# A hybrid decoder trunk on one core: weights stationary for the lora, k, r and v projections, three rounded passes for r1, v and the A blocks

## The chip, the cores and the metric

One core of a Trainium2 chip. The metric is the device time of one execution in microseconds; the median of three runs before the change is 2560.14 us (2558.58 to 2572.45). Engine names in the rows: PE is TensorE's matmul, PEld its weight load, DVE is VectorE, ACT ScalarE, POOL GpSimd, SP SyncE, which here only issues transfers.

## The reference

256 positions of width 2048 go through two layers. Layer 0 is what the change touches:

```python
h = rmsnorm(x, g_pre_mix) * (1 + sc_m) + sh_m      # shift/scale from c @ w_ada ("adaLN")
z = h @ w_in_ab                                    # 2048 -> 2*1024 (A: u, v) + 5 parts for B
y_a = chunked_spatial_gating(z[..., :2048], ...)   # gelu, layernorm of v, 128x128 causal mixing
y_b = rwkv7_time_mix(z[..., 2048:], ...)           # r, k, v of 1024; lora parts of 64, 64, 160
y = concatenate([y_a, y_b]) @ w_out_ab
x = x + gt_m * rmsnorm(y, g_post_mix)
```

`rwkv7_time_mix` begins with a token shift, `z + mu * (z_prev - z)`, where `z_prev` is z one position earlier. Then decay, gates and a delta-rule state update over the positions follow. Each layer has a SwiGLU feed-forward behind it, layer 1 has attention in place of A and B. All is in 32-bit floats.

## The kernel before, in words

**Ways to multiply.** A *rounded* matmul uses fp32r operands: a 32-bit value is split into a rounded high half and a rest, and a product is made of three passes (high x high, high x low, low x high). `load_split` loads one step of weights (256 rows of K by 512 columns, 512 KB, buffers `w32`, four of them) and splits it: a copy on ScalarE (`wh`, line 191) and a subtraction on VectorE (`wl`, line 192), both issued at a raised priority. `dense` multiplies so. `dense32` (line 893) multiplies the same step with plain floats, `xT` stationary and the weights moving, and splits nothing. One plain-float matmul shows as two records in the trace, a rounded one as one.

**First stage (lines 410 to 469).** x comes transposed (`xT`, features on partitions). Shift and scale of the pre-norm are dots of `cond` (silu of c on every partition) with strips of `w_ada`, 1 MB each: `strips(j)` loads four of them through six scratch buffers in turn (`slots`) and VectorE dots each with `cond` (`ada_dot`, line 117), giving the shift and scale of two K tiles. `h_rows(j)` applies them on ScalarE. Then the weights of lora (288 columns), k0, k1 and r0 for these two K tiles are loaded into two sets of scratch buffers (`wslots`) and multiplied into eight banks of PSUM. j runs from 0 to 7. All these transfers go through SP's queue in the order of the program; x, `cond` and the small tables come through ScalarE's queue. Position lies on the partitions of the results, so ScalarE copies them to scratch (`zn_tiles`, line 469).

**Second stage.** The main stream is seven blocks of `dense32`, eight steps each: r1, v0, v1 (the rest of B), then two blocks of A's v and two of A's u; then `w_out` for A's half (4 blocks of 4 steps, `dense`), and after that for B's half. A background generator, `rk_gen`, holds all of B's work in pieces, each with a credit; `pump`, called after every step, releases pieces at 1.8 credits a step (3 in its last part) and one or more adaLN strips of later sublayers (`ada_gen`, 512 KB each, two buffers, one dot on VectorE each). The piece order of `rk_gen`: lora transposes and shift (line 495), sigmoids and decay (`E`), `to_T("k")`, key normalisation, `to_T("r")`, bonus, `to_T("v")`, scores `SCN` and `SRA`, a triangular inversion of 31 sequential steps on VectorE (lines 669 to 674), then the four chunks of the state update and group norm, ending in `YB`. `to_T` (line 527) transposes a block of k, r or v on TensorE, 128 by 128 (line 539), and applies the token shift: a scaled copy on ScalarE and one or two multiply-adds on VectorE. The second half of `w_out` needs `YB`.

**Order.** The framework lays instructions out engine by engine before the run, by priority (program order, with the splits raised) among what its own estimate holds ready; on the chip each engine and each queue then runs its list strictly in order. Big scratch tiles share slots by tag: `H0`, `H1` and `X` hold one tile each at a time, a new owner waiting for the old one's last reader.

Of the kernel before, what the change touches and what calls it, by code (L numbers as in the profile page):

```python
# [7 lines left out]
F32 = mybir.dt.float32  # L8
F32R = mybir.dt.float32r
# [42 lines left out]
def trunk(ctx: ExitStack, tc, io, out, dbg=None):  # L52
# [32 lines left out]
    om = cpool.tile([P, 27], F32, name="om")  # L85
    V.tensor_scalar(om, cols[:, COLS["mu_k"][0]:COLS["mu_l"][1]], -1.0, 1.0, op0=OP.mult, op1=OP.add)
    oka = cpool.tile([P, 8], F32, name="oka")
    V.tensor_scalar(oka, cols[:, COLS["k_a"][0]:COLS["k_a"][1]], -1.0, 1.0, op0=OP.mult, op1=OP.add)

# [271 lines left out]
    def split_from(ps_ap, h_ap, l_ap):  # L361
# [4 lines left out]
    EX = hpool.tile([P, KT, S], F32, tag="H0", name="EX")  # L366
# [18 lines left out]
    EXf = EX.rearrange("p k s -> p (k s)")  # L385
    slots = [KBf[:, 0:D], KBf[:, D:2 * D], SCf[:, 0:D], SCf[:, D:2 * D], EXf[:, 0:D],
             EXf[:, D:2 * D]]
# [4 lines left out]

# [3 lines left out]
    def nat(flat_ap, i, ncol):  # L396
        return flat_ap[:, i:i + NT * ncol].rearrange("p (t n) -> p t n", t=NT)

    lora, win = io["w_lora"], io["w_in"]
    zn_tiles = {"lora": nat(ATf, 0, 288), "k0": nat(RAf, 2048, 512), "k1": nat(RAf, 3072, 512),  # L400
                "r0": nat(RAf, 0, 512), "r1": nat(RAf, 1024, 512),
                "v0": nat(VTf, 0, 512), "v1": nat(VTf, 1024, 512)}
# [5 lines left out]
    with tc.tile_pool(name="spool", bufs=1) as sp:  # L408
# [30 lines left out]
        def h_rows(j, cc):  # L439
            for k in range(2):  # L440
                kt = 2 * j + k
                A.activation(xT[:, kt, :], xT[:, kt, :], AF.Identity, bias=cc[:, 0, k:k + 1],
                             scale=cc[:, 1, k:k + 1])

        def bank(pool, nm):
# [5 lines left out]
               "r0": [bank(ps_ms, "ms") for _ in range(NT)]}  # L451
        for j in range(KT // 2):
            cc = strips(j)
            if j == 0:
                for k4 in range(4):
                    ks = slice(4 * k4, 4 * k4 + 4)
                    V.tensor_tensor(xT[:, ks, :], xT[:, ks, :], rb4, op=OP.mult)
# [20 lines left out]
    E = hpool.tile([P, 2, 8, S], F32, tag="H0", name="E")  # L478
    have = {"lora", "k0", "k1", "r0"}
# [6 lines left out]
    def rk_gen():  # L486

        while "lora" not in have:
            yield None
        zn = zn_tiles["lora"]  # L490
        zl = lp.tile([P, 3, S], F32, tag="gbu", name="zl")
        for f, w in ((0, P), (1, P), (2, 32)):
            ps = msbank()
            for t in range(NT):
                T.transpose(ps[:w, tsl(t)], zn[:, t, f * P:f * P + w], ident)
            A.activation(zl[:w, f, :], ps[:w, :S], AF.Copy, scale=omu("l", f)[:w])
            V.scalar_tensor_tensor(zl[:w, f, 1:S], ps[:w, 0:S - 1], col("mu_l", f)[:w],
                                   zl[:w, f, 1:S], op0=OP.mult, op1=OP.add)
            yield 0.8
# [27 lines left out]
        def to_T(name, dst):  # L527
            for b in range(2):
                while f"{name}{b}" not in have:
                    yield None  # L530
                zn = zn_tiles[f"{name}{b}"]
                pss = []
                for i2 in range(2):
                    ps = msbank()
                    psv = ps.rearrange("p (g s) -> p g s", g=2)
                    for i in range(2):
                        f = 2 * i2 + i
                        for t in range(NT):
                            T.transpose(psv[:, i, tsl(t)], zn[:, t, f * P:(f + 1) * P], ident)
                    pss += [psv[:, 0], psv[:, 1]]  # L540
                for i in range(4):
                    g, z = 4 * b + i, pss[i]
                    mu = col("mu_" + name, g)
                    if name == "k":
                        A.activation(dst[:, g], c4(z), AF.Copy, scale=omu(name, g))
                        V.scalar_tensor_tensor(dst[:, g, 0, 1:64], z[:, 0:63], mu,
                                               dst[:, g, 0, 1:64], op0=OP.mult, op1=OP.add)
                        V.scalar_tensor_tensor(dst[:, g, 1:4, :],
                                               z[:, 63:255].rearrange("p (c t) -> p c t", c=3), mu,
                                               dst[:, g, 1:4, :], op0=OP.mult, op1=OP.add)  # L550
                    else:
                        A.activation(dst[:, g, :], z, AF.Copy, scale=omu(name, g))
                        V.scalar_tensor_tensor(dst[:, g, 1:S], z[:, 0:S - 1], mu, dst[:, g, 1:S],
                                               op0=OP.mult, op1=OP.add)
                    if i % 2:
                        yield 0.8

        R_, Kk = RA[:, 0], RA[:, 1]
        K_, B_ = KB[:, :, :, 0, :], KB[:, :, :, 1, :]

        def c4(a):
            return a.rearrange("p (c t) -> p c t", c=4)

        yield from to_T("k", K_)


# [30 lines left out]
        yield from to_T("r", R_)  # L597
# [19 lines left out]
        yield from to_T("v", VT)  # L617
# [5 lines left out]
        SRA = hpool.tile([P, 64, 64], F32, tag="H1", name="SRA")  # L623
# [255 lines left out]
        YB = hpool.tile([P, 2, 8, S], F32R, tag="H1", name="YB")  # L879
# [13 lines left out]
    def dense32(wsrc, evac):  # L893
        ps = [ps_mm.tile([P, 512], F32, name="mm") for _ in range(NT)]
        for ch in range(KT // 2):
            w = wpool.tile([P, 2, 512], F32, tag="w32", name="w32", bufs=4)
            SY.dma_start(w, wsrc(ch))
            for k in range(2):
                kt = 2 * ch + k
                for t in range(NT):  # L900
# [5 lines left out]
    def evac_z(nm):  # L906
        def f(ps):
            for t in range(NT):
                A.activation(zn_tiles[nm][:, t, :], ps[t], AF.Copy)
            have.add(nm)  # L910
        return f

    for nm, src, ncol in first[4:]:
        dense32(src, evac_z(nm))
# [383 lines left out]
```

## Time and profile before

| | |
|---|---|
| median of 3 runs | 2560.14 us (2558.58 to 2572.45) |
| the profiled execution | 2557.72 us, its span 2555.7 us |
| TensorE matmul busy | 2429.3 us, 95% of the span |
| TensorE weight load busy | 1860.5 us, 73% |
| VectorE busy | 1619.6 us, 63% |
| ScalarE busy | 1037.1 us, 41% |
| GpSimd busy | 102.0 us, 4% |
| transfers | 623.47 MB, mean 244 GB/s |

The trace's times are microseconds from the start of the span. A window's row gives how long each engine was busy in it. A group's row gives a line of the kernel, the engine, the operation, tiles out<-in with their shapes, how many there were, their busy time, the mean length of one in ns, and the engine's idle time just before them with what ended it. Matmuls are pipelined, so the length of one is not its pace: the pace is read from starts, or from a merged run of them.

### The profile page before, as it was taken

The page shows a single profiled execution, that of the slowest core. Times are in us where ns is not written, and L with a number is a line of the kernel's source. Part 1 is how long each engine was busy: PE and PEld are TensorE (multiplying, and loading weights), DVE is VectorE, ACT ScalarE, POOL GpSimd, SP SyncE. Part 2 cuts the span into 40 slices and gives each one's busy share as a digit, 9 for nine tenths or more (in the row PEclk, how much of TensorE's full clock was granted, in tenths as well). Part 3 has the DMA queues.
Part 4 walks back from the last instruction along what each step waited for, and adds up shares of the span by engine and source line. Part 5 has one row for each costly group of instructions (what it writes and reads, how often), then busy time and mean ns, then how long its engine had stood idle before and what let it go on. Part 6 is the DMA issues. An engine that isn't in the chain of part 4 may idle for free. (4 is left out here: it accounts for less than half of the span.)

```text
span 2555.7 us, 29570 instructions
## 1 busy us (share of the span) xinstructions
PE 2429.3 (95%) x10944; PEld 1860.5 (73%) x10944; DVE 1619.6 (63%) x2176; ACT 1037.1 (41%) x1423; POOL 102.0 (4%) x83
## 2 busy tenths in 40 slices
PE   4998989998999999999998999999899999999998
PEld 2443537677887777888887777778778888888886
DVE  5656794568877777654446778865776455444444
ACT  1042103347443443444445444446544444444443
POOL 0002210001000000000001001100100000000000
PEclk8998999899999999999999999999999999999999
DMA  9987776574988888755554888855587555556554
GB/s 377 417 302 242 259 245 212 177 265 146 329 317 306 317 296 310 234 205 191 193 193 146 302 292 311 300 196 206 201 318 265 188 190 189 189 190 206 191 194 151
DMA packets 166528, 623.47 MB, mean 244 GB/s; under 512 B 18560, under 2 KB 18752, under 8 KB 161392
## 3 DMA queue, kind: packets, MB, share of 16 engines
q1 hardware_dynamic: 164288, 612.74, 68.7%
q10 hardware_dynamic: 2096, 8.86, 0.9%
q8 instruction: 85, 1.39, 0.2%
q14 instruction: 59, 0.48, 0.1%
HBM read 619.39 MB, written 2.13 MB: 243 GB/s over the span
## 5 line engine op out<-in xcount | busy, mean ns | idle before, releaser
L192 DVE TENSOR_TENSOR wl<-w,wh 128x1024 fp32r<-128x1024 f32 x688 | 836.8, 1223 | 532.9 <-ACT wh L191 531.7
L191 ACT ACTIVATE wh<-w 128x1024 fp32r<-128x1024 f32 x688 | 728.3, 1059 | 1005.4 <-PE mm L205 941.7
L117 DVE SCALAR_TENSOR_TENSOR ada<-ada,cond 128x1024 f32<-128x1024 f32 x320 | 392.9, 1229 | 286.1 <-DMA ada<-in_w_ada_dram 285.2
L204 PE MATMUL mm<-wl,hF 128*128 128x512 f32 x1408 | 552.4, 392 | 15.0 <-DVE wl L192 14.8
L203 PE MATMUL mm<-wh,hF 128*128 128x512 f32 x1408 | 552.9, 393 | 0.0
L205 PE MATMUL mm<-wh,hFl 128*128 128x512 f32 x1408 | 549.9, 391 | 0.0
L204 PEld LDWEIGHTS mm<-wl,hF 128*128 128x128 f32 x1408 | 264.5, 188 | 81.8 <-DVE wl L192 28.6
L205 PEld LDWEIGHTS mm<-wh,hFl 128*128 128x128 f32 x1408 | 264.4, 188 | 54.5
L203 PEld LDWEIGHTS mm<-wh,hF 128*128 128x128 f32 x1408 | 264.5, 188 | 53.7
L204 PE MATMUL mm<-wl,aH 128*128 128x512 f32 x704 | 276.9, 393 | 0.0
L205 PE MATMUL mm<-wh,aL 128*128 128x512 f32 x704 | 275.5, 391 | 0.0
L203 PE MATMUL mm<-wh,aH 128*128 128x512 f32 x704 | 274.6, 390 | 0.0
L901 PE MATMUL mm<-w,xT 128*128 128x512 f32 x448 | 216.3, 630 | 4.6 <-DMA w<-in_w_in_dram 4.6
L901 PEld LDWEIGHTS mm<-w,xT 128*128 128x128 f32 x448 | 86.2, 201 | 105.9 <-issue 97.7
L203 PE MATMUL mm<-wh,hA 128*128 128x512 f32 x384 | 155.7, 405 | 0.0
L204 PE MATMUL mm<-wl,hA 128*128 128x512 f32 x384 | 152.3, 397 | 3.1 <-DVE wl L192 3.1
L203 PEld LDWEIGHTS mm<-wh,aH 128*128 128x128 f32 x704 | 132.2, 188 | 30.1
L204 PEld LDWEIGHTS mm<-wl,aH 128*128 128x128 f32 x704 | 132.3, 188 | 28.6
L205 PEld LDWEIGHTS mm<-wh,aL 128*128 128x128 f32 x704 | 132.3, 188 | 27.7
L205 PE MATMUL mm<-wh,hAl 128*128 128x512 f32 x384 | 150.8, 393 | 0.0
L204 PEld LDWEIGHTS mm<-wl,hA 128*128 128x128 f32 x384 | 72.8, 190 | 20.1 <-DVE wl L192 6.3
L205 PEld LDWEIGHTS mm<-wh,hAl 128*128 128x128 f32 x384 | 72.7, 189 | 15.1
(312 smaller groups left out, 2049.5 us busy)
## 6 DMA issues: line engine op xcount, KB each, us to landing
w<-in_w_ffn_in_dram SPq DMA_DIRECT2D x352, 512.0 KB, 3.9
ada<-in_w_ada_dram SPq DMA_DIRECT2D x320, 512.0 KB, 5.1
w<-in_w_ffn_out_dram SPq DMA_DIRECT2D x176, 512.0 KB, 3.6
w<-in_w_qkv_dram SPq DMA_DIRECT2D x96, 512.0 KB, 5.2
w<-in_w_in_dram SPq DMA_DIRECT2D x56, 512.0 KB, 5.2
w<-in_w_out_dram SPq DMA_DIRECT2D x32, 512.0 KB, 3.8
w<-in_w_o_dram SPq DMA_DIRECT2D x32, 512.0 KB, 3.3
KB<-in_w_ada_dram SPq DMA_DIRECT2D x12, 1024.0 KB, 12.0
```

Source lines behind the costliest of these rows:

```text
L117: V.scalar_tensor_tensor(w, w, 1.0, cond[:, k0:k0 + n], op0=OP.mult, op1=OP.mult, accum_out=dst)
L191: A.activation(wh[:, :, :ncol], w32[:, :, :ncol], AF.Copy)
L192: V.tensor_sub(wl[:, :, :ncol], w32[:, :, :ncol], wh[:, :, :ncol].bitcast(F32))
L203: T.matmul(o, h, wh[:, k, :ncol], start=(kt == 0), stop=False)
L204: T.matmul(o, h, wl[:, k, :ncol], start=False, stop=False)
L205: T.matmul(o, l, wh[:, k, :ncol], start=False, stop=(kt == nkt - 1))
L901: T.matmul(ps[t], xT[:, kt, tsl(t)], w[:, k, :], start=(kt == 0), stop=(kt == KT - 1))
```

## The change

- Lora, k0, k1 and r0 are multiplied with the weights stationary, in pieces of 128 columns (lora 128, 128, 32), and `xT` moving, 256 positions wide. So columns land on partitions, and the token shift reads PSUM directly (`shift`, `shift4`, and a loop for lora). `to_T`, the transposes, `zn_tiles` and the copies to them are gone. The shifts of lora, k and r0 stand before the background generator, which then waits for r1 and v1 only.
- r1, v0 and v1 become `dense_T`: weights split by `load_split` and stationary, `XH` and `XL` (the split of h, made in `h_rows`) moving, 256 columns, three rounded passes.
- The four A blocks become `dense` with three rounded passes of 512 columns.
- `strips(0)` stands before the loop and `strips(j+1)` before the weights of set j. There are five strip buffers instead of six.
- Two small operations on the column table (`om`, `oka`) move behind the first stage; scratch tiles change tags (`XH`, `XL` take `H0`, `H1`; `E`, `SRA`, `YB` go to `X`; `YA` to `H0`, `YP` to `H1`).

```diff
-    EX = hpool.tile([P, KT, S], F32, tag="H0", name="EX")
...
-    slots = [KBf[:, 0:D], KBf[:, D:2 * D], SCf[:, 0:D], SCf[:, D:2 * D], EXf[:, 0:D],
-             EXf[:, D:2 * D]]
+    slots = [KBf[:, 0:D], KBf[:, D:2 * D], SCf[:, 0:D], SCf[:, D:2 * D], ATf]
...
+            ks = slice(2 * j, 2 * j + 2)
+            A.activation(XH[:, ks, :], xT[:, ks, :], AF.Copy)
+            V.tensor_sub(XL[:, ks, :], xT[:, ks, :], XH[:, ks, :].bitcast(F32))
...
+        nxt = strips(0)
...
         for j in range(KT // 2):
-            cc = strips(j)
...
+            cc = nxt
             h_rows(j, cc)
+            if j + 1 < KT // 2:
+                nxt = strips(j + 1)
             for i, (nm, src, ncol) in enumerate(first[:4]):
                 w = wslots[j % 2][i][:, :2 * ncol].rearrange("p (k n) -> p k n", k=2)
                 SY.dma_start(w, src(j))
+                nf = -(-ncol // P)
                 for k in range(2):
                     kt = 2 * j + k
-                    for t in range(NT):
-                        T.matmul(acc[nm][t][:, :ncol], xT[:, kt, tsl(t)], w[:, k, :],
-                                 start=(kt == 0), stop=(kt == KT - 1))
-        for nm, src, ncol in first[:4]:
-            for t in range(NT):
-                A.activation(zn_tiles[nm][:, t, :ncol], acc[nm][t][:, :ncol], AF.Copy)
+                    for f in range(nf):
+                        n = min(P, ncol - f * P)
+                        T.matmul(acc[nm][f // 2][:n, (f % 2) * S:(f % 2 + 1) * S],
+                                 w[:, k, f * P:f * P + n], xT[:, kt, :],
+                                 start=(kt == 0 and f % 2 == 0),
+                                 stop=(kt == KT - 1 and (f % 2 == 1 or f == nf - 1)))
...
+        else:
+            A.activation(dst[:, g, :], z, AF.Copy, scale=omu(name, g))
+            V.scalar_tensor_tensor(dst[:, g, 1:S], z[:, 0:S - 1], mu, dst[:, g, 1:S],
+                                   op0=OP.mult, op1=OP.add)
...
+    def dense_T(wsrc, name, b):
+        ps = [ps_mm.tile([P, 512], F32, name="mm") for _ in range(2)]
         for ch in range(KT // 2):
-            w = wpool.tile([P, 2, 512], F32, tag="w32", name="w32", bufs=4)
-            SY.dma_start(w, wsrc(ch))
+            wh, wl = load_split(wsrc(ch), 512)
             for k in range(2):
                 kt = 2 * ch + k
-                for t in range(NT):
-                    T.matmul(ps[t], xT[:, kt, tsl(t)], w[:, k, :], start=(kt == 0),
-                             stop=(kt == KT - 1))
+                for f in range(4):
+                    o = ps[f // 2][:, (f % 2) * S:(f % 2 + 1) * S]
+                    fs = slice(f * P, (f + 1) * P)
+                    T.matmul(o, wh[:, k, fs], XH[:, kt, :], start=(kt == 0 and f % 2 == 0),
+                             stop=False)
+                    T.matmul(o, wh[:, k, fs], XL[:, kt, :], start=False, stop=False)
+                    T.matmul(o, wl[:, k, fs], XH[:, kt, :], start=False,
+                             stop=(kt == KT - 1 and f % 2 == 1))
             pump(AR, BR)
-        evac(ps)
...
+        shift4(name, b, ps, tgt[name])
+        have.add(f"{name}{b}")
...
-        dense32(src, evac_z(nm))
+        dense_T(src, nm[0], int(nm[1]))
...
-        dense32(lambda ch, b=b: win[6 + b, ch], evac_av(b))
+        dense(lambda ch, b=b: win[6 + b, ch], KT, *hl(XH, XL), 512, evac_av(b), AR, BR)
...
-        dense32(lambda ch, b=b: win[8 + b, ch], evac_au(b))
+        dense(lambda ch, b=b: win[8 + b, ch], KT, *hl(XH, XL), 512, evac_au(b), AR, BR)
```

## Rows read from the trace of the kernel before

**Rows 1.** Windows: length, busy PE PEld DVE ACT POOL, PEclk, DMA share, GB/s.
```profile
57.87:134.30 76.43, 73.87 (x193) 36.23 (x191) 47.63 (x50) 5.89 (x12) 0.00 (x0) 1.00 1.00 408
134.30:146.65 12.35, 12.35 (x33) 6.19 (x33) 3.97 (x7) 4.25 (x8) 0.52 (x1) 1.00 0.91 329
146.65:312.40 165.75, 156.07 (x512) 77.56 (x510) 110.47 (x215) 49.53 (x94) 29.63 (x31) 0.95 0.76 259
312.40:381.50 69.10, 57.40 (x129) 24.74 (x129) 62.96 (x120) 6.20 (x10) 13.65 (x6) 0.96 0.75 252
381.50:500.00 118.50, 116.32 (x1104) 77.01 (x1105) 59.64 (x101) 40.77 (x69) 0.00 (x0) 0.88 0.60 197
500.00:553.00 53.00, 49.10 (x280) 39.27 (x279) 42.14 (x66) 20.68 (x28) 0.00 (x0) 0.94 0.70 240
```

**Rows 2.** Waits of TensorE, 146 to 500: us in total, times, longest.
```profile
PE ms L690 <- DVE AT L683: 9.3, 2, 7.1
...
PE mm L901 <- DMA w<-in_w_in_dram: 4.6, 2, 2.4
```

**Rows 3.** Timeline of TensorE: start, length, operation, count [idle before, releaser].
```profile
158.47 2.75 PE L511 MATMUL ms<-tz,w2a 128*128 128x256 f32 x12
...
171.38 10.46 PE L901 MATMUL mm<-w,xT 128*128 128x512 f32 x24
181.68 1.04 PE L539 MATMUL ms<-cst,RA 128*128 128x128 f32 x8
...
397.61 2.05 PE L958 MATMUL ms<-vA,wsT 128*128 128x128 f32 x16
...
526.85 0.39 PE L203 MATMUL mm<-wh,YA 128*128 128x512 f32 x1
...
529.57 0.39 PE L203 MATMUL mm<-wh,YA 128*128 128x512 f32 x1
```

**Rows 4.** Groups by shape, 146.65 to 553: busy, mean ns, idle before.
```profile
L117 DVE SCALAR_TENSOR_TENSOR ada<-ada,cond 128x1024 f32<-128x1024 f32 x107 | 132.1, 1239 | 90.8 <-DMA ada<-in_w_ada_dram 90.4
...
L192 DVE TENSOR_TENSOR wl<-w,wh 128x1024 fp32r<-128x1024 f32 x14 | 16.8, 1217 | 3.2 <-ACT wh L191 3.2
L191 ACT ACTIVATE wh<-w 128x1024 fp32r<-128x1024 f32 x15 | 15.8, 1056 | 22.4 <-PE mm L205 14.4 <-DMA w<-in_w_out_dram 5.7 <-DVE ada L117 2.3
...
L958 PEld LDWEIGHTS ms<-vA,wsT 128*128 128x128 f32 x32 | 3.8, 191 | 0.4 <-issue 0.3
...
L545 ACT ACTIVATE KB<-ms,om 128x256 f32<-128x256 f32 x8 | 3.5, 466 | 7.4 <-DVE KB L548 7.4
...
L548 DVE SCALAR_TENSOR_TENSOR KB<-ms,cols,KB 128x192 f32<-128x192 f32 x8 | 3.3, 408 | 0.0
...
L884 DVE TENSOR_TENSOR YB<-RA,YB 128x512 fp32r<-128x512 f32 x4 | 2.5, 687 | 0.2 <-ACT YB L883 0.2
```

**Rows 5.** Timeline of VectorE and GpSimd in the inversion.
```profile
330.32 0.34 DVE L672 TENSOR_TENSOR AT<-AT,KBn 128x175 f32<-128x175 f32 x1
...
360.04 4.20 POOL L942 TENSOR_TENSOR vA<-vA,gn 128x1024 f32<-128x1024 f32 x1 [41.50 <-DVE vA L941]
...
361.96 2.48 DVE L672 TENSOR_TENSOR AT<-AT,KBn 128x175 f32<-128x175 f32 x1
```

**Rows 6.** Timeline of the first stage, TensorE and VectorE.
```profile
23.75 0.18 DVE L86 TENSOR_SCALAR om<-cols 128x27 f32<-128x27 f32 x1 [22.68 <-DMA cols<-in_cols_dram]
...
43.05 4.21 PE L465 MATMUL ms<-RA,xT 128*128 128x288 f32 x8 [17.06 <-ACT xT L442]
...
57.87 2.10 PE L465 MATMUL ms<-vA,xT 128*128 128x288 f32 x8
...
108.94 2.29 DVE L117 SCALAR_TENSOR_TENSOR KB<-KB,cond 128x2048 f32<-128x2048 f32 x1 [4.45 <-DMA KB<-in_w_ada_dram]
...
119.78 2.21 PE L465 MATMUL ms<-RA,xT 128*128 128x288 f32 x8 [0.55 <-ACT xT L442]
...
123.53 2.29 DVE L117 SCALAR_TENSOR_TENSOR EX<-EX,cond 128x2048 f32<-128x2048 f32 x1 [4.44 <-DMA EX<-in_w_ada_dram]
...
134.30 2.21 PE L465 MATMUL ms<-vA,xT 128*128 128x288 f32 x8 [2.02 <-ACT xT L442]
...
138.08 1.23 DVE L117 SCALAR_TENSOR_TENSOR ada<-ada,cond 128x1024 f32<-128x1024 f32 x1 [4.46 <-DMA ada<-in_w_ada_dram]
```

More of the change, by code (lines that the diff above doesn't have):

```diff
@@ new lines, in trunk, with c4, shift @@
+    om = cpool.tile([P, 27], F32, name="om")
+    V.tensor_scalar(om, cols[:, COLS["mu_k"][0]:COLS["mu_l"][1]], -1.0, 1.0, op0=OP.mult, op1=OP.add)
+    oka = cpool.tile([P, 8], F32, name="oka")
+    V.tensor_scalar(oka, cols[:, COLS["k_a"][0]:COLS["k_a"][1]], -1.0, 1.0, op0=OP.mult, op1=OP.add)
+    have = {"lora", "k0", "k1", "r0"}
+    def c4(a):
+        return a.rearrange("p (c t) -> p c t", c=4)
+    def shift(name, g, z, dst):
+        mu = col("mu_" + name, g)
+        if name == "k":
+            A.activation(dst[:, g], c4(z), AF.Copy, scale=omu(name, g))
+            V.scalar_tensor_tensor(dst[:, g, 0, 1:64], z[:, 0:63], mu, dst[:, g, 0, 1:64],
+                                   op0=OP.mult, op1=OP.add)
+            V.scalar_tensor_tensor(dst[:, g, 1:4, :],
+                                   z[:, 63:255].rearrange("p (c t) -> p c t", c=3), mu,
+                                   dst[:, g, 1:4, :], op0=OP.mult, op1=OP.add)
+        else:
+            A.activation(dst[:, g, :], z, AF.Copy, scale=omu(name, g))
+            V.scalar_tensor_tensor(dst[:, g, 1:S], z[:, 0:S - 1], mu, dst[:, g, 1:S],
+                                   op0=OP.mult, op1=OP.add)
@@ new lines, in shift4 @@
+    def shift4(name, b, banks, dst):
+        for i in range(4):
+            shift(name, 4 * b + i, banks[i // 2][:, (i % 2) * S:(i % 2 + 1) * S], dst)
+    zl = lp.tile([P, 3, S], F32, tag="gbu", name="zl")
+    for f, w in ((0, P), (1, P), (2, 32)):
+        z = acc["lora"][f // 2][:w, (f % 2) * S:(f % 2 + 1) * S]
+        A.activation(zl[:w, f, :], z, AF.Copy, scale=omu("l", f)[:w])
+        V.scalar_tensor_tensor(zl[:w, f, 1:S], z[:, 0:S - 1], col("mu_l", f)[:w],
+                               zl[:w, f, 1:S], op0=OP.mult, op1=OP.add)
@@ L470, in trunk @@
+    tgt = {"k": KB[:, :, :, 0, :], "r": RA[:, 0], "v": VT}
+    for nm in ("k0", "k1", "r0"):
+        shift4(nm[0], int(nm[1]), acc[nm], tgt[nm[0]])
     A.dma_start(indT, io["indT"])
@@ L477, in trunk @@
     A.dma_start(w2a2, io["w2a2"])
-    E = hpool.tile([P, 2, 8, S], F32, tag="H0", name="E")
-    have = {"lora", "k0", "k1", "r0"}
+    E = hpool.tile([P, 2, 8, S], F32, tag="X", name="E")
     pp_cm = tc.tile_pool(name="pp", bufs=1)
@@ L486, in rk_gen @@
     def rk_gen():
[L488 to L493, printed above, removed]
-            for t in range(NT):
[L495 to L499, printed above, removed]
         A.activation(tz[0:64, 0, :], zl[0:64, 0, :], AF.Tanh)
@@ L596, in rk_gen @@
             yield 1.0
-        yield from to_T("r", R_)
+        while "r1" not in have:
+            yield None
         dump("r", R_)
@@ L616, in rk_gen @@
             yield 0.5
-        yield from to_T("v", VT)
+        while "v1" not in have:
+            yield None
         dump("RA", RA)
@@ L878, in rk_gen @@
         yield from group_norm(slice(192, 256), 8)
[L879 removed]
+        YB = hpool.tile([P, 2, 8, S], F32R, tag="X", name="YB")
         rk["YB"] = YB
@@ L980, in trunk @@
     wout = io["w_out"]
-    YP = hpool.tile([P, NT, D], F32, tag="H0", name="YP")
+    YP = hpool.tile([P, NT, D], F32, tag="H1", name="YP")
     def evac_yp(b):
```

65 lines of the change are left out of this document (7 added, 58 removed).

## The prediction

> **What bounds the kernel now.** I read the page's engine table first: TensorE is busy for 95% of the span, VectorE 63%, ScalarE 41%. So TensorE is the engine to follow, but the change touches only the first 553 us or so, and there the average says little. So I cut that stretch into windows [rows 1]. The reader is to see three different limits. From 57.87 to 134.30 the DMA share is 1.00 at 408 GB/s: the transfers bound. From 146.65 to 312.40 and from 381.50 to 500.00 TensorE is busy 156.1 of 165.8 us and 116.3 of 118.5 us: it bounds. From 312.40 to 381.50, where the triangular inversion runs, VectorE is busy 63.0 of 69.1 us and TensorE only 57.4: VectorE bounds. The waits of TensorE [rows 2] say the same: the longest one is on the inversion's transposes.
>
> Then I looked at what a piece of weights costs (a "step" below is 256 rows of K of one 512-wide block, 8 steps to a block, 7 blocks = 56 steps in the stage after 146.65). A plain-float matmul of 512 columns is two records. 24 records take 10.46 us, less about 0.16 us by which the last one outlasts the pace: 0.429 us each, so a step (8 records) is 3.43 us and a block 27.5 us [rows 3].
>
> **First stage, 0 to 146.65.** Its transfers set it. The first dot of each set of four strips stands 14.59 us after that of the set before (108.94 to 123.53), and 4.45 us of that is VectorE waiting while the four weight pieces of the set pass [rows 6]. TensorE needs only 12.35 us for a set (134.30 to 146.65, [rows 1]), and late in the stage it waits for it (0.55 and 2.02 us, [rows 6]).
> - Lora with its weights stationary: 2 K tiles x 3 matmuls of 256 columns = 12 records. Records of 256 plain-float columns cost (2.75 - 0.16)/12 = 0.216 us [rows 3], so 2.59 us, against 2.10 - 0.16 = 1.94 us for the eight records of 288 columns [rows 6]: +0.65 us a set. K and r keep their 1024 columns per K tile, in twice as many matmuls at half the price: nothing. The set becomes 13.0 us, still below 14.59.
> - Strips one step ahead: the bytes are the same, so the last piece lands when it did (the first thing behind it is ready at 138.08). But on SP's queue the weights of set j are now moved behind the strips of set j+1, so weights of set 6 start to land only after the last strips. Those land 4.45 us sooner than now: 131.1 (123.53 plus three quarters of 14.59 - 4.45) less 4.45 = 126.6. From about 127.3 TensorE still has two whole sets, 26.0 us, and ends at 153.3 instead of 146.65: +6.6. Today it has one set left after the last strips. On the other side, the two small operations on the column table no longer stand ahead of the first dot: VectorE waited 22.68 us for that table and started at 23.75 [rows 6]. That lets TensorE begin before 43.05, frees weight buffers sooner, and can take back the few us in which the queue was not full. Five strip buffers instead of six make SP wait for a dot before the fourth strip of a set, with everything behind it on SP; at a strip per 2.5 us three are still in flight, so I put nothing. Bounds -3 (weights slip ahead of the strips where those wait) to +12 (another set late); I take **+5**.
> - Splitting h (a copy on ScalarE, a subtraction of 0.69 us on VectorE, [rows 4], 8 times) lies beside transfers: VectorE is busy 47.6 of 76.4 us there [rows 1]. Without that cover it would be 8 x 0.69 = 5.5 us. The subtraction waits for the copy, and behind it stand the dots of the next set, which at this point have not landed.
> - The shifts now read PSUM at the end of the stage, and r1 waits for the banks of k0 and k1 until they have: per 128 columns a ScalarE copy of 0.47 us and two VectorE operations of at most 0.41 [rows 4]. Those of k0 and most of k1 run while TensorE multiplies k1 and r0 (3.4 us each), so 0; without that cover k1's four, 3.3 us. The adaLN dots and lora's shift stand beside them on VectorE.
>
> **Second stage, TensorE's side.** A rounded 512-column matmul costs (529.57 - 526.85)/12 = 0.227 us [rows 3]; an A step is 12 of them, 2.72 us, 0.71 less than now. The r1, v0, v1 steps are 24 rounded matmuls of 256 columns, each with weights of its own. The trace has none. The nearest row in length of streaming with fresh 128x128 weights is the spatial-gating matmul: 16 records in 2.05 us, (2.05 - 0.16)/16 = 0.118 us [rows 3]. Bounds: half of 0.227 = 0.113 below, and above the whole load of weights laid bare, 0.191 us [rows 4]. I take 0.120: 2.88 us a step, 0.55 less than now. Transposes that go: 48 for k, r and v in 12 groups of 8 records at 1.04 - 0.16 = 0.88 us [rows 3], 10.5 us, and six records of lora, 0.7 us.
>
> The Trainium skill ("TensorE: Matmul & The Clock Gate", section on LDWEIGHTS) puts a load at its columns over 1.2 GHz, which for 128 columns is an estimated 107 ns, as long as 256 rounded columns stream; a load that did not hide would by that rule make 0.21 us a matmul and each of these blocks 13 us dearer than now. The gating row, with as long a load beside as short a stream, stands against it.
>
> **Second stage, VectorE's side.** Each of 56 steps now needs a split: 1.22 us on VectorE, 1.06 on ScalarE [rows 4]: 68 and 59 us. Evacuations of 0.6 us on ScalarE go, and the token shifts are the same operations, started earlier. What can give way: 107 adaLN dots of 1.24 + 0.08 us = 141 of the 275 us of VectorE from 146.65 to 553 [rows 1, 4], which run ahead of their readers. By stretch:
> - 146.65 to 312.40 (24 r/v steps, 6 A steps): TensorE loses 24 x 0.55 + 6 x 0.71 + 11.2 = 28.7 us. VectorE goes from 110.5 to 110.5 + 30 x 1.22 = 147 us in what would be 137, so either about 20 dots give way or TensorE waits. ScalarE, with table loads and sigmoids at the start, gets 32 us more. Bounds -28.7 and 0; I take two thirds, **-19**.
> - 312.40 to 381.50 (16 A steps): TensorE's 16 x 0.71 = 11.4 us are worth nothing while VectorE bounds. VectorE gets 16 x 1.22 = 19.5 us: 63.0 + 19.5 = 82.5, +13.4, if the dots keep coming one to a step. If all 16 give way, 82.5 - 21.1 = 61.4: -7.7. Splits go ahead of other VectorE work in the order, and the weights of a step stand on SP behind a dot's strip, so some of both: **+5**.
> - 381.50 to 500.00 (10 A steps): TensorE bounds, VectorE has half its time free: 10 x 0.71 = **-7** (bounds -9 and -3; the granted clock is 0.88 there).
> - After 500: the same instructions, background work some three steps earlier in the order because its transposes took credits; scratch tiles change their slots, and each new owner is written after the old one's last reader by data dependence already. 0, bounds -4 and +4.
>
> VectorE also shares something with GpSimd. In the inversion, a product of 175 columns takes 0.34 us alone and 2.48 us beside a GpSimd multiplication [rows 5]. Dots, which like the new splits read two operands from the buffer, average 1.24 against the split's 1.22 [rows 4]: 0.02 x 56 = 1 us, which I leave in the bounds.
>
> The Trainium skill ("SBUF — State Buffer", section "Who interferes with whom") says that a VectorE instruction with two inputs in SBUF and a GpSimd instruction that reads it exclude each other for a whole instruction, whoever comes second waiting. The slow products agree; by that rule a seventh or so of the splits could be held back by an estimated 1 us each, 8 us in all, in stretches where they stand before TensorE, and the sum would be -8.
>
> **Sum.** +5 - 19 + 5 - 7 = -16 on the profiled execution's 2557.72 us (its span 2555.7 plus 2.0 around it): 2541.7. The median of the runs shown, 2560.14, stands 2.4 above it, so **2544**.
>
> **Rivals.**
> - TensorE keeps all its gain: the dots step aside everywhere. +5 - 28.7 - 7.7 - 7 = -38, so 2522. For it: half of VectorE's work can wait. Against it: weights stand behind adaLN strips on SP's queue, and TensorE already waits for weights [rows 2].
> - VectorE becomes the bound (the slower side). From 146.65 to 381.50 it has 173.4 us; with 46 splits, 229.5. If it reaches only the share it has where it bounds now, 63.0/69.1 = 0.911, that takes 252 us instead of 234.9, +17; with +5 and -7, +15: 2575. Decides if fewer than some ten dots give way there; each that does returns 1.3 us. For it: the inversion is one long chain. Against: the dots.
> - Weight loads show in the 256-column matmuls: 0.191 instead of 0.120 us, 192 x 0.071 = 13.6 us a block, three blocks, +41: 2585. Decides from about 0.17 us a matmul. Against it: the gating row.
> - The strips are not a step ahead: SP's queue is filled in the old order because four of a set need buffers of the set before. Only lora remains of the first stage, 0.65 a set where TensorE is late, +1: 2540.
>
> **How the numbers follow.** Forecast 0.40 (own range 2530 to 2558), TensorE keeps all 0.17, VectorE bounds 0.21, weight loads 0.12, no step ahead 0.10. A measurement of this kernel can tell about 0.5%, 12.8 us, from no change: faster means below 2547.3, slower above 2572.9. Faster: 0.26 of the forecast, 0.17, 0.07 of the last = 0.50. Same: 0.14, 0.08 of VectorE's, 0.02 and 0.03 = 0.27. Slower: 0.13 + 0.10 = 0.23. The range, 2512 to 2580, reaches past the first two rivals and leaves out part of the third and the full sum of the lower bounds.
>
> **What would show it.** The last matmul of the first stage near 152 rather than 147; 256-column rounded matmuls 0.12 us apart; VectorE above 90% up to the end of the inversion with fewer than 107 dots before the output projection's second half; TensorE waiting there for the low half of the split. A stage after the first that shortens by less than 8 us, or matmuls 0.17 us apart, would make it wrong.

## The result: slower, by about 23 us

The changed kernel takes 2582.81 us (median of 5 runs, 2579.73 to 2585.91) against 2560.14 before: ratio 1.0083, 95% interval 1.0061 to 1.0106. The forecast was 2544. The profiled execution has a span of 2584.2 us against 2555.7. TensorE is busy for 2421.4 us instead of 2429.3, VectorE for 1689.2 instead of 1619.6. So TensorE is busy for 8 us less, not for the some 40 that the forecast's rows take from it, and the kernel takes longer.

Of what was to show the steps, these came true: 256-column matmuls 0.12 us apart, VectorE above 90% up to the inversion's end, 90 dots instead of 107 between the first stage and the second half of w_out, TensorE waiting for the split's low half. The first stage's end (155.4, not 152) and the stage behind it, which was to be over 8 us shorter and is longer, did not.

First, windows of the changed kernel, cut where its stages end: first stage, then to the first matmul behind the inversion, to the first of w_out, to the end of its first half, to the first of the FFN. Columns as in [rows 1].

```profile
44.57:155.38 110.81, 110.81 (x480) 86.96 (x481) 77.86 (x101) 25.32 (x45) 0.53 (x1) 0.98 0.95 379
155.38:394.97 239.59, 205.71 (x1170) 173.45 (x1169) 217.62 (x346) 100.53 (x137) 48.97 (x37) 0.93 0.73 248
394.97:505.40 110.43, 103.98 (x1143) 81.31 (x1143) 58.08 (x106) 37.83 (x68) 0.00 (x0) 0.73 0.37 121
505.40:553.95 48.55, 46.78 (x215) 38.10 (x213) 37.37 (x52) 21.34 (x27) 0.00 (x0) 1.00 0.83 294
553.95:639.30 85.35, 55.64 (x216) 41.24 (x216) 70.35 (x110) 39.07 (x79) 3.40 (x2) 0.88 0.76 264
```

The same cuts of the kernel before, where [rows 1] have others:

```profile
43.05:146.65 103.60, 101.04 (x257) 50.05 (x257) 66.03 (x74) 11.89 (x22) 0.52 (x1) 0.98 0.98 393
146.65:381.50 234.85, 213.47 (x639) 102.30 (x638) 173.43 (x334) 55.73 (x104) 43.28 (x37) 0.95 0.76 257
381.50:501.40 119.90, 117.47 (x1113) 77.93 (x1113) 61.04 (x102) 41.45 (x71) 0.00 (x0) 0.88 0.60 197
501.40:563.60 62.20, 58.55 (x316) 47.03 (x316) 46.78 (x70) 24.64 (x32) 0.00 (x0) 0.95 0.70 242
563.60:620.40 56.80, 48.62 (x219) 40.01 (x217) 43.01 (x63) 37.55 (x77) 3.48 (x2) 0.94 0.53 186
```

Read them in pairs. The first stage ends 8.7 us later, and TensorE is busy in all of it. The second takes 4.7 us more although TensorE has 7.8 us less to do in it: VectorE has 44 us more. How far one profile is from another shows in e14 below, which runs the code of before up to w_out: its first stage ends 1.4 us later than before and its second takes 3.2 us more. So what is clear of the second stage is that it did not get shorter. The third is 9.5 us shorter, at a granted clock of 0.73 (a mean of the two levels, 1.2 and 2.4 GHz) where before had 0.88. The last two take 133.9 us instead of 119.0, and the whole excess lies in the last. Sum to the FFN's first matmul: +18.9 us. Another 9.6 us come after it, in code that the change does not touch.

Where TensorE waits in the changed kernel, 155 to 505 (us in total, times, longest), the answer to [rows 2]:

```profile
PE ms L674 <- DVE AT L667: 14.8, 2, 12.7
PE mm L199 <- DVE wl L187: 13.0, 7, 4.6
PE mm L889 <- DVE wl L187: 3.9, 2, 2.0
```

L674 is L690 of before, the first matmul behind the inversion. TensorE's timeline shows what the longest of these waits means (its last two lines), and above that parts of the first stage's last two sets and the first new matmuls:

```profile
138.54 3.62 PE L459 MATMUL ms<-xT,RA 128*128 128x256 f32 x16
141.99 3.19 PE L459 MATMUL ms<-xT,vA 128*128 128x256 f32 x12
145.11 3.72 PE L459 MATMUL mm<-xT,vA 128*128 128x256 f32 x16
...
155.69 0.28 PE L888 MATMUL mm<-XL,wh 128*128 128x256 f32 x1
155.81 0.28 PE L889 MATMUL mm<-XH,wl 128*128 128x256 f32 x1
155.92 0.28 PE L886 MATMUL mm<-XH,wh 128*128 128x256 f32 x1
...
381.88 0.39 PE L200 MATMUL mm<-wh,XL 128*128 128x512 f32 x1
394.97 3.59 PE L674 MATMUL ms<-AT,SCN 32*32 32x32 f32 x64 [12.70 <-DVE AT L667]
```

The last A matmul starts at 381.88; before, it stood at 491.8. The blocks that the change made cheaper are finished 110 us earlier, and then TensorE has nothing in its queue that may run until VectorE has finished the inversion. What VectorE does from A's first matmul to there (busy, mean ns, idle before):

```profile
L187 DVE TENSOR_TENSOR wl<-w,wh 128x1024 fp32r<-128x1024 f32 x34 | 45.8, 1346 | 0.2
L112 DVE SCALAR_TENSOR_TENSOR ada<-ada,cond 128x1024 f32<-128x1024 f32 x31 | 38.2, 1236 | 7.6 <-DMA ada<-in_w_ada_dram 7.4
```

All 32 A splits, and the first three of w_out, stand in front of the inversion's end, not 22 A splits as forecast.

In the second half of w_out, SyncE's queue: what its issues wait for, 505 to 640 in the changed kernel, then 505 to 620 before.

```profile
SPq L122 <- DVE ada L112: 71.6, 30, 7.7
SPq L182 <- DVE wl L187: 18.0, 12, 3.1
```
```profile
SPq L187 <- DVE wl L192: 67.3, 32, 4.6
SPq L127 <- DVE ada L117: 21.8, 8, 6.9
```

Before, the queue waited for the weights' own buffers. Now it waits for the buffers of adaLN strips, which a dot must free, and the weights stand behind them. Two stretches of the changed kernel's timeline, SyncE's issues and the matmul that waited for one of them:

```profile
565.32 0.42 SPq L182 DMA_DIRECT2D w<-in_w_out_dram  x1
569.11 3.95 SPq L122 DMA_DIRECT2D ada<-in_w_ada_dram  x2
573.11 0.90 SPq L182 DMA_DIRECT2D w<-in_w_out_dram  x2
```
```profile
573.85 1.22 PE L198 MATMUL mm<-wh,YB 128*128 128x512 f32 x2 [10.35 <-ACT wh L186]
```

Dots by stretch, counted by their start: 4 in the first stage, then 65, 30, 12 and 0 before (to the inversion's end, to w_out, in its two halves); 3, then 53, 24, 13 and 21 now.

### The profile page after: what moved, and what is told of

Read it like the earlier page. It is cut to its first block, busy times and chain, and to the rows that moved or that the text cites. A ratio compares the mean times of both kernels' runs of the same rounds, so it can differ in the third digit from the quotient of the medians.

```text
span 2584.2 us, 31106 instructions
## 1 busy us (share of the span) xinstructions
PE 2421.4 (94%) x11626; PEld 1966.5 (76%) x11626; DVE 1689.2 (65%) x2240; ACT 1090.6 (42%) x1472; POOL 106.1 (4%) x83
## 5 line engine op out<-in xcount | busy, mean ns | idle before, releaser
L186 ACT ACTIVATE wh<-w 128x1024 fp32r<-128x1024 f32 x744 | 787.9, 1060 | 1135.2 <-PE mm L200 975.2
L187 DVE TENSOR_TENSOR wl<-w,wh 128x1024 fp32r<-128x1024 f32 x744 | 910.9, 1231 | 535.3 <-ACT wh L186 533.9
L198 PEld LDWEIGHTS mm<-wh,hA 128*128 128x128 f32 x384 | 73.4, 191 | 14.4
L1101 POOL TENSOR_SCALAR dh<-cst 128x384 f32<-128x384 f32 x16 | 28.7, 1795 | 1027.0 <-PE mm L200 748.0
```

The lines of the kernel that those rows point to most:

```text
L186: A.activation(wh[:, :, :ncol], w32[:, :, :ncol], AF.Copy)
L187: V.tensor_sub(wl[:, :, :ncol], w32[:, :, :ncol], wh[:, :, :ncol].bitcast(F32))
L198: T.matmul(o, h, wh[:, k, :ncol], start=(kt == 0), stop=False)
L1101: G.tensor_scalar(dh, alibi, slope, None, op0=OP.mult)
```

## Experiments

Each run is compared with runs of the kernel before on the same chip; the ratio is to these, with its 95% interval. The changed kernel's own is 1.0083 (1.0061 to 1.0106). Where a run's interval overlaps with that one (e3, e5, e7, e9, e11, e13, e17), its time is not told apart from the changed kernel's, and what it tells is read from its stages. "The inversion's end" is the first matmul behind it (395.0 us in the changed kernel, 381.5 before).

**e1 to e4: is it VectorE?**

e1, no split at all:
```
 dense_T: w = wpool.tile(...); SY.dma_start(w, wsrc(ch)); T.matmul(o, w[:, k, fs], xT[:, kt, :])
 A blocks: dense32 as before;  E, SRA, YB, YA, YP in the slots of before;  no XH, XL
```


> r1 and v keep their stationary weights but in plain fp32, the A blocks go back to plain fp32, no split of the input rows; the first stage stays as changed. Theory 1 (the 56 added weight splits, 74 us of VectorE between 155 and 384 us, delay the background chain, and the dots they displaced come due in the second half of w_out): the last half of w_out takes 43 to 48 us again instead of 70.9, the inversion ends at 383 to 390 us instead of 395.0, and the time is 2552 to 2570 us. Theory 2 (the loss is the first stage's and the stationary form's, not the splits'): the second half of w_out stays above 60 us, time 2575 to 2595.

Measured: 2557.48 us, ratio 0.9986 (0.9958 to 1.0013); the matmuls of the last half of w_out 43.8 us; the inversion's end 368.6, earlier than either theory had it. Theory 1 holds on the time.

e2, VectorE lighter (no low half is made; the third pass reads the high half again):
```
-            V.tensor_sub(wl[:, :, :ncol], w32[:, :, :ncol], wh[:, :, :ncol].bitcast(F32))
-        return wh, wl
+            if low: V.tensor_sub(wl[:, :, :ncol], w32[:, :, :ncol], wh[:, :, :ncol].bitcast(F32))
+        return (wh, wl) if low else (wh, wh)
```


> The seven blocks r1, v and A run as changed, but their weight splits leave out VectorE's subtraction (the low part; the third pass reads the high part again), so TensorE's passes are the same and VectorE has 56 instructions of 1.33 us, 74 us, less. Theory 1 (VectorE's splits): inversion ends 10 or more us earlier (375 to 385), second half of w_out 43 to 50 us, time 2545 to 2562. Theory 2 (the order of evacuations and the first stage): the inversion ends at 390 to 395, time 2575 to 2585.

Measured: 2552.96 us, ratio 0.9971 (0.9951 to 0.9992), inversion's end 340.4, far earlier than expected. But from the end of w_out's first half to the FFN it still took 83 us, with 20 dots in it. That part of theory 1 was wrong: the splits of the seven blocks are not what is slow there.

e3, TensorE lighter (one of the three passes is left out):
```
-                    T.matmul(o, wh[:, k, fs], XL[:, kt, :], start=False, stop=False)
 (and the like in the A blocks)
```


> The seven blocks leave out one of their three passes (high weights times low part of the rows): TensorE has 56 x 8 matmuls of 256 or 4 of 512 columns less, some 53 us, and VectorE and ScalarE do all that they did. Theory 1 (TensorE's time no longer sets this stage): the inversion ends within 4 us of 395, the time stays at 2575 to 2590. Theory 2 (TensorE still sets it): the inversion ends 25 to 50 us earlier and the time is 2530 to 2560.

Measured: 2575.93 us, ratio 1.0055 (1.0034 to 1.0076), inversion's end 390.0 (5 us, theory 1 had 4 at most). Some 53 us taken from TensorE are worth 7 us at most, not clear of noise; the 74 us taken from VectorE in e2 were worth 30.

e4, dots halved (half of each product is left out):
```
+ n = 512 if layer == 0 and s < 5 else 1024      # dma_start and ada_dot of n columns
```


> The adaLN dots of the second, third and fourth modulation rows that layer 0 needs (and the fifth's none) load and multiply 512 instead of 1024 columns, so half of that product is left out: 128 dots at most of 1.24 us become some 0.7 us, about 30 us of VectorE less before the inversion's end and 10 less in the second half of w_out, and half their transfers. Theory 1 (dots that came due late fill VectorE and the load queue in the second half of w_out): this half takes 43 to 55 us instead of 70.9, the inversion ends at 378 to 388, time 2545 to 2565. Theory 2 (that half is slow for its own order of loads and splits): still over 62 us, time 2570 to 2583.

Measured: 2542.52 us, ratio 0.9932 (0.9906 to 0.9957), inversion's end 371.6, and 56.9 us from the first matmul of w_out's second half to the FFN's, where the changed kernel has 85.35. Both effects belong to the dots, as theory 1 said. The inversion's end and the time came out below its ranges.

**e5 and e6: which of the blocks?** E takes SCN's place in both, so that `xT`, `XH` and `XL` can live side by side.
```
e5: r1, v plain (dense_T of e1), A rounded      e6: r1, v rounded, A plain (dense32)
+    E = SCf.rearrange("p (x g s) -> p x g s", x=2, g=8)
+        rn = pp.tile([16, S], F32, name="rn")
```


> r1 and v in plain fp32 with stationary weights, the A blocks in three rounded passes as changed (the decay and boost rows E take SCN's place, which is empty then): 32 of the 56 added splits remain, 42 us of VectorE. By the run without VectorE's share of the splits, 74 us of it are worth 30 us of time, and by the one with a pass less, 53 us of TensorE are worth 7. Theory 1 (VectorE's load, whoever brings it): 24 splits less give 13 us, 24 plain steps cost 2: 2566 to 2576, inversion ends at 372 to 388. Theory 2 (it is r1 and v that hurt, as the background waits for them): nearly all comes back, 2550 to 2560, inversion at 365 to 372.

> The other half: r1 and v in three rounded passes as changed, the A blocks in plain fp32 (E again in SCN's place): 24 splits remain, 32 us of VectorE. Theory 1 (VectorE's load, whoever brings it): 32 splits less give 17 us, 32 plain steps cost 3: 2562 to 2573, inversion ends at 365 to 382. Theory 2 (r1 and v hurt): 2575 to 2585, inversion at 385 to 395.

Measured: e5 2582.19 us, ratio 1.0081 (1.0054 to 1.0108), inversion's end 407.2. e6 2559.71, ratio 0.9997 (0.9977 to 1.0017), inversion's end 354.2. Both theories fall: VectorE's load does not count alike whoever brings it, and r1 and v do not hurt at all. The A blocks bring the whole loss. Windows from A's first matmul to the inversion's end, in e1, e6, e5, the changed kernel, e2 and the kernel before:

```profile
276.67:368.65 91.98, 88.41 (x290) 45.34 (x289) 79.15 (x160) 9.95 (x19) 9.09 (x10) 0.96 0.80 272
```
```profile
262.60:354.20 91.60, 86.38 (x290) 43.99 (x289) 78.51 (x161) 9.95 (x19) 9.25 (x10) 0.98 0.76 262
```
```profile
272.15:407.21 135.06, 112.32 (x514) 89.33 (x513) 125.21 (x198) 47.27 (x57) 18.82 (x12) 0.92 0.75 258
```
```profile
259.70:394.97 135.27, 109.54 (x514) 86.94 (x513) 128.11 (x207) 46.51 (x55) 18.63 (x12) 0.93 0.77 265
```
```profile
252.60:340.40 87.80, 72.77 (x383) 60.06 (x382) 78.35 (x153) 32.03 (x41) 17.89 (x12) 0.95 0.80 279
```
```profile
267.65:381.50 113.85, 99.97 (x329) 50.37 (x328) 93.37 (x177) 12.65 (x25) 19.75 (x12) 0.96 0.76 256
```

Two sizes are read here. Rounded r1 and v let A begin at 262.6 instead of 276.7: 14.1 us gained, forecast as 24 x 0.55 = 13.2. Rounded A blocks make the stretch to the inversion's end 43 us longer, 135 instead of 92, and VectorE is busy for 93 to 95% of it. These 43 us answer to the splits that now stand there, 34 with 45.8 us in the changed kernel and, in e5, these:

```profile
L187 DVE TENSOR_TENSOR wl<-w,wh 128x1024 fp32r<-128x1024 f32 x34 | 48.4, 1423 | 3.1 <-ACT wh L186 3.1
```

That it is VectorE's part of the split, and not TensorE's passes, ScalarE's copies or the scratch tiles' new places, e2 shows: it keeps these three, leaves out the subtraction alone, and the stretch is 88 us. So a split before the inversion's end costs its full length if it stands where VectorE is the one that is waited for (A), and nothing where it is TensorE (r1, v).

e2 shows one thing more. A steps that started before the inversion's end are 32 of 32 in the changed kernel, in e3 and in e5, but 21 in e2, with TensorE's passes as short as in the changed kernel, and 23 before.

**e7, e8, e17: the first stage.**
```
e7:  n, a = P, min(f * P, ncol - P);  T.matmul(..., w[:, k, a:a + n], xT[:, kt, :])
e8:  first stage as changed; r1, v through dense32 and to_T, A through dense32, as before
e17: cc = strips(j) in step j, ahead of its weights, as before
```


> The changed kernel with lora's third piece as 128 columns (160 to 288) in place of 32, so that all first-stage matmuls have one form; the 32 outputs wanted then lie on partitions 96 to 127. Theory 1 (the 32-column form costs 0.53 us a set): first stage ends at 150.5 to 152 instead of 155.4, time 2574 to 2582. Theory 2 (lora's records cost 0.26 us for another reason, such as the bank that they add to): it ends at 155 to 156, time 2580 to 2585.

> Only the first stage as changed (lora, k, r0 with stationary weights, strips one step ahead); r1 and v come as rows and are transposed, A in plain fp32, as before the change. Theory 1 (the first stage costs its 8.7 us, and the transposes of lora, k and r0 that go are worth part of it): 2558 to 2568, that is the run without splits plus 0 to 8. Theory 2 (stationary weights of r1 and v are themselves a loss): 2545 to 2556, less than the run without splits.

> The changed kernel with each set's four strips loaded and multiplied in its own step again, not one step ahead; the rest as changed. Theory 1 (TensorE, never waiting between 44.57 and 155.38, sets this stage, so the order of the strips is worth little): it ends within 3 us of 155.4, time 2578 to 2590. Theory 2 (the strips ahead hide a wait that comes back): 160 to 172, time 2588 to 2600; theory 3 (they delay the weights): 150 or less.

Measured: e7 ends the first stage at 151.4 us, time 2577.82, ratio 1.0054 (1.0037 to 1.0072): theory 1. Lora's twelve records in it take 141.25 - 138.66 = 2.59 us, not 3.12:

```profile
138.66 2.75 PE L459 MATMUL ms<-xT,vA 128*128 128x256 f32 x12
141.25 3.62 PE L459 MATMUL mm<-xT,vA 128*128 128x256 f32 x16
```

e17 ends it at 153.5, time 2583.36, ratio 1.0100 (1.0069 to 1.0131): the order of the strips is worth nothing, theory 1. e8: 2565.77, ratio 1.0017 (0.9996 to 1.0039), within theory 1; the first stage by itself is not told apart from no change.

**e9 and e11: is it the order of the queues?**
```
e9:  Bg.rate = 3  ->  Bg.rate = 1.5   (chunk loop and group norms)
e11: with tc.high_priority(PRI) -> priority 0 for the splits of the seven blocks
```


> The changed kernel with the chunk loop and the group norms recorded at half the pace beside the main steps (Bg.rate 1.5 in place of 3), so that the spatial gating, YA and most of the first half of w_out stand before the chunk loop's end on TensorE's queue, not behind it; no work is added or left out. Theory 1 (TensorE's gain is lost because what follows the main blocks is queued behind the background's chain): the first w_out matmul comes at 430 to 470 us instead of 505.4, time 2545 to 2570. Theory 2 (the chain itself sets the end, its order does not matter): 2577 to 2590.

> The changed kernel with the splits of r1, v and the A blocks recorded without their priority of 50, so that VectorE's queue has them behind background work recorded earlier. Theory 1 (32 A splits pushed in front of the inversion delay it by nearly their own 42 us): inversion ends at 355 to 375 us instead of 395.0, time 2555 to 2575. Theory 2 (the scheduler orders them so anyway): within 4 us of 395 and 2583.

Measured: e9 2588.27 us, ratio 1.0104 (1.0073 to 1.0134); e11 2583.77, ratio 1.0091 (1.0061 to 1.0122), inversion's end 393.4. My theory 1 fell in both; their times lie in theory 2's ranges. In e9 w_out's first matmul came at 487.6, not before 470, and the chunk loop's results (YB) 28 to 33 us later than in the changed kernel, so the second half of w_out began at 554.9, where it had begun at 554.0. In e11 the splits stand in the same places without their priority.

**e10, dots from another queue:**
```
+ q = G if layer == 0 and s < 5 else SY;  q.dma_start(w, io["w_ada"][...])
```


> The changed kernel with the strips of layer 0's second to fourth modulation rows (96 dots) issued from GpSimd's queue instead of SyncE's, so that a weight load never stands behind a strip that waits for its buffer. Theory 1 (the second half of w_out is slow because its weight loads stand behind strips on SyncE's queue): it takes 44 to 55 us instead of 70.9, time 2562 to 2572. Theory 2 (it is slow because VectorE is full there, or the transfers are): still 62 us or more, 2576 to 2590.

Measured: 2627.74 us, ratio 1.0273 (1.0235 to 1.0311), outside both. On GpSimd's empty queue 35 of the strips came during the first stage and took its transfers; TensorE waited 9.6 to 12.5 us for each of the last four sets there, and the stage ended at 212 us. Two of these waits:

```profile
115.99 5.05 PE L460 MATMUL ms<-xT,RA 128*128 128x256 f32 x12 [11.36 <-DMA RA<-in_w_lora_dram]
142.49 5.47 PE L460 MATMUL ms<-xT,vA 128*128 128x256 f32 x12 [10.89 <-ACT xT L428]
```

No dot was left for the second half of w_out, and its matmuls took 43.8 us as before. So this run does not tell the queue from the dots.

**e12 to e16 and e18: the late dots, and a version that is faster.**
```
e13, e14:  dense(... wout[b, 4 + ch] ..., evac_yb(b), 1 -> 0, quiet=...)    in the kernel after / before
e12 = e6 + e7 + Bg.rate 1.5;   e15 = e12 + the edit of e13
e16 = e15 with e1's plain r1 and v;   e18 = e15 with Bg.rate 3
```


> r1 and v in rounded passes, A in plain fp32 as in the run with A plain, the wide third piece of lora, and the chunk loop recorded at 1.5. The run with A plain had 2559.7; the wide piece gives 4 to 5, the later chunk loop 10 to 30 if theory 1 holds: 2530 to 2548. If only the wide piece counts: 2553 to 2558.

> The changed kernel, but the 16 steps of the second half of w_out record no dots: the 16 or so dots of the fifth modulation row that stood there, which nothing needs before the middle of the FFN, come in the FFN's steps. No work is left out. Theory 1 (dots that came late fill this half): from the last matmul of the first half to the FFN's first it takes 62 to 74 us instead of 86.4, time 2562 to 2574. Theory 2 (the load and split of the weights themselves): 82 to 88 us, 2578 to 2588.

> The same edit in the kernel before the change, where no dot ran in the second half of w_out at all. Both theories: within 4 us of before, 2556 to 2564; 10 us less would say that these dots cost something else.

> r1 and v rounded, A in plain fp32, wide third piece of lora, chunk loop recorded at 1.5, and no dots recorded in the second half of w_out. The run without the last edit had 2551.4, and 80 us from the last matmul of the first half of w_out to the FFN. Theory 1: 62 to 70 us there, time 2533 to 2543. Theory 2: 76 to 82 us, 2547 to 2555.

> The same with r1 and v in plain fp32 too (no split anywhere before w_out). Theory 1 (r1 and v's rounded passes are worth 14 us at the inversion once no dots take it back): 5 to 14 us more than the run with them rounded, 2542 to 2555. Theory 2 (their gain is lost in any case, since TensorE has the A blocks' plain passes left): the same as that run within 4 us.

> The version with r1 and v rounded, A plain, wide lora piece and no late dots, but the chunk loop recorded at its old pace of 3. Theory 1 (with plain A blocks TensorE has work beside the chunk loop either way): within 4 us of the version's 2537. Theory 2 (the later recording lets the first half of w_out run beside the chunk loop): 2542 to 2556, first w_out matmul at 485 or later instead of 460.6.

Measured: e12 2551.38 us, 0.9965 (0.9946 to 0.9983), between its two answers. e13 2574.48, 1.0059 (1.0042 to 1.0077), at the edge of theory 1. e14 2557.12, 0.9990 (0.9972 to 1.0007), no change, as both had it. e15 2536.83, 0.9913 (0.9884 to 0.9942), theory 1. e16 2539.80, 0.9919 (0.9893 to 0.9945), theory 2. e18 2541.72, 0.9936 (0.9911 to 0.9961), between its two. The last half of w_out with the way to the FFN, in e13 and in e15:

```profile
552.90:625.80 72.90, 53.11 (x218) 40.88 (x217) 56.29 (x86) 38.91 (x80) 3.40 (x2) 0.88 0.67 227
```
```profile
525.00:589.70 64.70, 51.03 (x218) 41.10 (x216) 51.29 (x76) 37.83 (x78) 3.48 (x2) 0.92 0.66 238
```

In the changed kernel this stretch took 85.35 us, before 56.80. So the 12 dots that e13 moves are 12 of the 28 us. Nine are left there in e13 and six in e15. Over all runs, the matmuls of that half take 43.8 us where at most five dots run between its first matmul and the FFN's (before, e1, e8, e10, e14, e16, e18, and e4 with eight half dots), 51.6 with six (e15), 54.7 to 62.1 with nine to eighteen (e5, e6, e12, e13), and 66 to 72 with twenty to twenty-two (the changed kernel, e2, e3, e7, e9, e11, e17). Time and dots go together; since other things differ between these runs too, that is not the price of one dot. e15 beats both kernels, the one before by about 22 us (0.0087 of 2559.78). That it owes this to r1 and v's rounded passes or to the later chunk loop is not shown: e16 and e18 lack one of these each, and their intervals overlap its own. What all three share is plain A blocks, the wide lora piece and no dots recorded in the second half of w_out.

## Why the prediction was wrong

| step | forecast | measured | told apart by |
|---|---|---|---|
| first stage | +5 (-3 to +12) | +8.7 | e7: 4.0 of it; e17: strips none |
| second stage to the inversion's end | -19 + 5 | +4.7 | e2, e5, e6 |
| from there to w_out | -7 | -9.5 | |
| w_out to the FFN | 0 (-4 to +4) | +14.9 | e13: about 13 of it |
| the rest | 0 | +9.6 in the profile | open |

**The step that failed is the inversion: "312.40 to 381.50 ... +5", with "What can give way: 107 adaLN dots" behind it.** Its rows were right: VectorE bounds there, a split costs 1.2 to 1.35 us. From A's first matmul to the inversion's end the forecast's rows make about +2 us (two thirds of six cheaper A steps, and the +5); measured are 135.27 instead of 113.85, +21.4. Two things in it were not right. First, I laid the splits out along the old timeline, 6 A steps ahead of the inversion, 16 beside it and 10 behind it. All 32 ran ahead of the inversion's end, where their splits cost 43 us. (Without them that stretch would have been shorter than before: 92 us in e1 and e6.) Why the order came out so is not shown. It is not the cheaper passes alone, since 21 steps ran ahead in e2, nor the raised priority of the splits (e11); that each split delays the inversion, and a later end leaves room for more A steps ahead of it, would fit. Second, dots did give way, 12 of the 65, as I had hoped for some; but I priced a dot that gives way at zero. It still has to run, on the same queue as weights: by the start of w_out 80 had run instead of 99 (3 + 53 + 24 against 4 + 65 + 30), and 21 came in the second half of w_out. Few of them were due there. The FFN's norm needs 96, of which three were left; the other 18 belong to a row that is read only behind the FFN's first half, and stood there because the order had them next. That is the row "After 500: ... 0, bounds -4 and +4". From w_out's first matmul to the FFN's, e13 takes 13 of the 14.9 us away by an edit that gains nothing before the change (e14); in the time its gain is not clear of noise.

**First stage.** The size was near by luck, the mechanism was not. I had it bound by transfers, with the strips' new place on SyncE's queue costing 6.6 us. The window shows TensorE busy for 110.81 of 110.81 us, and e17 shows the strips' place to be worth 1.9 us there, little more than e14 differs from before, and nothing in the time. What I missed is lora's 32-column piece: I took its records at the price of a full one, 2.59 us a set, and they cost 3.12. A set is then 3.12 + 3 x 3.45 = 13.5 us of TensorE, 1.15 more than the 12.35 before; over eight sets that is 9.2, near the 8.7 measured. That the two small operations leave the head of VectorE's queue also brought nothing: TensorE starts at 44.57 instead of 43.05.

**r1 and v: right.** 256-column matmuls stand 0.12 us apart, so the rival of visible weight loads falls. By the price of a load in the Trainium skill ("TensorE: Matmul & The Clock Gate", section on LDWEIGHTS), a load laid bare would have made it an estimated 0.21; the trace shows no such sum. Its records of these loads are 0.19 us long, not an estimated 0.107, and they hide all the same. The 14.1 us at A's start are the forecast 13.2.

**After the inversion: right in size for another reason.** I forecast -7 by cheaper A steps. There were none left. Before, A blocks filled TensorE beside the chunk loop; now it runs the loop without them, and begins at this clock after 12.7 us without work (a window of the changed kernel):

```profile
394.97:398.50 3.53, 3.53 (x64) 3.46 (x64) 3.52 (x2) 0.59 (x1) 0.00 (x0) 0.50 0.00 0
```

That is the lower level, 1.2 GHz, and the whole stretch has a mean of 0.73 where before had 0.88. So the ten A steps of 3.43 us that I counted here, 34 us, are gone from the stretch, and it is 9.5 us shorter.

**The rivals.** "VectorE becomes the bound" is what happened. It had VectorE at 0.911 of the time to the inversion's end; it was 217.62 of 239.59, 0.908. Its price was 2575: it had +17 for the stage to the inversion's end, where 4.7 were measured, and nothing for the second half of w_out. Its condition (fewer than ten dots give way) was wrong: twelve did. "TensorE keeps all its gain" fails where the A blocks end at 382 and nothing follows. "No step ahead" had 2540; e17 takes the step ahead away and the time stays where it is.

The splits of the second stage are 1323 ns on average up to the inversion's end against 1217 in [rows 4], 57 x 0.106 = 6 us. Of all 59 up to there, the 47 that overlap no GpSimd instruction take 1216 ns on average, and the twelve that overlap one 1727. By the rule of the Trainium skill ("SBUF — State Buffer", section "Who interferes with whom") the prediction had an estimated 8 us. The trace agrees in size, with 12 x 0.51 = 6.1 us.

**Open.** The 9.6 us behind the FFN's first matmul. That code is the same in all these kernels (e14 has twelve dots more in it), and from there to the end the profiles have 1935.3 us (before), 1937.3 (e17), 1943.2 (e1), 1944.2 (e14), 1944.9 (after). The medians differ by 22.7 us, not by the profiles' 28.5, so part of it is which execution was profiled (for the changed kernel the slowest of its five). What makes the rest was not tried. Nor is it settled what each of the nine dots left in e13 costs, where 16 us more than before remain between the first half of w_out and the FFN; e15, with six, has 8.

## What to carry to other kernels

Work that is taken from one engine and given to another is priced at the place where the other is the one waited for: the same split cost nothing beside r1 and v and its full length beside the inversion. When the balance of the engines changes, lay out again what runs when: all 32 splits stood ahead of the inversion's end, where the kernel before had 23 of these steps. And work that can wait is not free: count where it will run instead, and what shares its queue there.

## What the runs showed of the hardware that I had not expected

- Twelve plain-float records of 256 columns take 3.12 us when four of them have 32 columns of weights, and 2.59 when all have 128 (e7): a narrow piece was dearer than a full one, by 0.53 / 4 = 0.13 us a record. In the trace of the changed kernel the next record starts 0.216 us after the last one between two full ones, 0.240 between two narrow ones, and 0.309 wherever the width changes.
- Rounded matmuls of 256 columns, each with fresh weights, run 0.12 us apart, half of the 0.227 of 512 columns.
- The first 64 small matmuls behind the inversion take 3.59 us after 12.7 us without work at a granted clock of 0.50. In the kernel before, after 7.1 us without work, they take 3.59 us too. In e15, after 2.4 us without work, they take 2.47 us at a clock of 0.83.
- A VectorE subtraction of 128x1024 took 1216 ns on average where no GpSimd instruction overlapped it and 1727 where one did. The two longest, 3.36 and 3.37 us, stand beside GpSimd operations of 2.4 and 2.5 us.
